# Head of a decoder step: prompt tokens loaded first, their squares on two engines, the new tokens' chain later

## The chip, the cores and the metric

The kernel runs on one core of a Trainium2 chip. The metric is the device time of one execution in microseconds (us); lower is better. A core has a matrix engine (TensorE, here PE, with its weight loads as PEld), a vector engine (VectorE, DVE), an activation engine (ScalarE, ACT), a general engine (GpSimd, POOL) and an engine that mostly issues DMAs (SyncE, SP). Each works through its own queue of instructions in order, and waits at an instruction until the semaphores that this instruction names have come far enough. Matmul results land in PSUM, everything else that the engines read or write lies in SBUF.

## The reference

One layer of a decoder is applied to 512 prompt tokens and to 8 new tokens, 1024 channels each. Only its first lines matter here:

```python
def rms_norm(x, g):
    y = xf * lax.rsqrt(jnp.mean(xf * xf, axis=-1, keepdims=True) + EPS)
    return (y * g.astype(F32)).astype(x.dtype)

def layer_step(r, ...):
    h = rms_norm(r, norm_mix_g)
    z = h @ w_in
    rq, rk, rv, rg, gq, gf, gi, gg, a_ret, a_hg = jnp.split(z, split_at, axis=-1)
    ...
```

Behind this stand a retention branch and an HGRN2 branch, the output projection, an MLP, a gated embedding and a final norm. All of that is the same in both kernels.

## The kernel before

All activations are held transposed, channels on partitions: `xT` (the tokens), and `hH` and `hL`, two parts whose sum is the normalised input h. A float32 matmul is made of three matmuls in a rounded format (fp32r): every operand is cut into a rounded part and a remainder (`hH`, `hL` for activations, `wh`, `wl` for weights), and the product is wh·hH + wh·hL + wl·hH. Eight channel blocks k of 128 and 520 token columns (512 prompt tokens, then the 8 new ones, `T:N`) make up one operand.

The weights come in **units** of 128 output columns: `load()` asks for the next unit's 512 KB (line 237, through SP's queue, into one of three `raw` buffers), and `prep()` cuts it into `wh` and `wl`, in halves or whole, on the engines that its argument names (first the engine of the rounding, then the engine of the subtraction), and asks for a later unit behind that. The program is in the order of the code; no scheduler reorders it.

The change concerns the head, lines 1415 to 1585 or so, up to the third unit:

- **Loads.** SP asks for the identity and ones (`cid`), the new tokens (`xs`, 8 x 1024), a stack of vectors (`rows`, 64 x 128, which holds the gains), and then for the four tiles of 128 prompt tokens (`xn`), with weight units between them.
- **Norm.** `normalized(x, m, c)` squares a tile on ACT and sums each row, forms 1/sqrt by Ln and Exp, and scales the tile on DVE (`xhat`). The new tokens go first, then tiles 0 and 1, later 2 and 3.
- **Transposes.** PE turns the raw tiles (`by_channel`, 4 blocks per PSUM bank; `keep` copies them to `xT` on DVE) and the scaled ones (`hat`, into four banks). `warm` issues transposes of the identity whose result nobody reads. The stack of vectors is turned too and copied to `cv`, whose columns are the gains by channel.
- **Rounding.** `cut(bs, k, half)` makes `hH` for 256 tokens of one block k on ACT, with the gain as scale, and `hL` on DVE.
- **First matmuls.** Units 0 and 1 are done in two halves of tokens (`OFS`: columns 0 to 255, then 256 to 519): `first_z(u, 0, 4)` does the first half of unit u, with the `wl` matmuls four blocks behind the others. Within unit 1's first half PE also turns the scaled tiles 2 and 3, and `cut` follows for the second half. Then both units' second halves run interleaved, with unit 1 two blocks behind.
- From `run_unit` of the third unit on (line 243 in the profile) all 520 columns are done at once.

The PSUM pool `pm` has two buffers of two banks (tiles named `m`). A new tile takes the older buffer, and its first writer waits for the last reader of what was there. Each of units 0 and 1 has one such tile for both its halves (`pp[u]`), so that unit 0 waits for the new tokens' results to be read out of `m0`, and unit 1 for `raws[1]`.

The new tokens' chain is: squares, Ln, Exp, scaling, eight small transposes of `xs` and eight of the scaled tile into `m0`, a copy to `xT`, the gain on DVE (`hd`), and the cut of its columns.

Of the kernel before, what the change touches and what calls it, by code (L numbers as in the profile page):

```python
# [45 lines left out]
def decoder_step_kernel(  # L46
# [1368 lines left out]
    dma(cid, unit_consts)  # L1415
# [4 lines left out]
    xn = []  # L1420
    for c in range(4):
        t = big.tile([128, D], F32, tag=f"S{12 + c}", name=f"xn{c}")
        dma(t, x_prompt[0, c * 128:(c + 1) * 128, :])
        xn.append(t)
        if c > 0:
            load()
# [16 lines left out]
    def normalized(x, m, c):

        r = ss5[0:m, c:c + 1]
        S.activation(junk[0:m], x, AF.Square, accum_out=r)
        S.activation(r, r, AF.Ln, scale=1.0 / D, bias=eps[0:m, 0:1])
        S.activation(r, r, AF.Exp, scale=-0.5)
# [1 line left out]
        V.tensor_scalar(t, x, r, None, op0=ALU.mult)  # L1450
        return t

# [30 lines left out]
    m0 = pm.tile([128, 2, 512], F32, tag="m", name="m")[:, 0]  # L1483
    for k in range(8):
        PE.transpose(m0[:, k * 8:k * 8 + 8], xs[:, k * 128:(k + 1) * 128], ident[0:8, 0:8])
    xh = normalized(xs, 8, 4)
    warm(8, m0[:, 192:320])
    raws = [pm.tile([128, 2, 512], F32, tag="m", name="m")]
# [2 lines left out]
    PE.transpose(m0[:, 128:192], rows, ident[0:64, 0:64])
# [6 lines left out]
    xhat.append(normalized(xn[1], 128, 1))
    keep(0, raws[0][:, 1], 1)
    V.tensor_copy(xT[:, :, T:N], m0[:, 0:64].rearrange("p (k t) -> p k t", k=8))  # L1500
    V.tensor_copy(cv, m0[:, 128:192])
    hd = pair("S1", "hd")[:, 0, 0:64].rearrange("p (k t) -> p k t", k=8)
    V.tensor_tensor(hd, m0[:, 64:128].rearrange("p (k t) -> p k t", k=8),
                    cv[:, V_MIX:V_MIX + 8].unsqueeze(2).to_broadcast([128, 8, 8]), op=ALU.mult)
# [8 lines left out]
    for k in range(8):
        cut(bs, k, 0)
        if k == 3:
            next(p1)
    keep(1, raws[1][:, 0], 0)
    keep(1, raws[1][:, 1], 1)
    xhat.append(normalized(xn[2], 128, 2))
# [148 lines left out]
```

## Time and profile before

| | us |
|---|---|
| median of 3 runs | 1088.36 (1088.34 to 1088.51) |
| the profiled execution | 1088.38 |
| its span, from the first to the last instruction | 1086.6 |
| PE busy in the first 20 us | 16.1 |
| ACT_TABLE_LOAD at the start, on ACT | 1.28 |
| waits of PE that a semaphore ended in the first 40 us, longest | 3.3, for the landing of xs |

The profile names an instruction by the line of the kernel that issued it and by tiles: `hL<-s,cv,hH` writes hL and reads s, cv and hH. A row of the timeline joins equal instructions that follow one another; "x8" is their count, and its time runs from the start of the first to the end of the last. A bracket at its end tells how long the engine had been idle before it and what ended that. PE's matmuls are pipelined, so a matmul's own length is more than the distance to the next one.

### The profile page before, as it was taken

How to read it: one execution, taken by the hardware profiler on the slowest of the kernel's cores; microseconds unless marked ns; L12 is line 12 of the kernel's file. 1: busy time of each engine (PE TensorE's matmuls, PEld its weight loads, DVE VectorE, ACT ScalarE, POOL GpSimd, SP SyncE). 2: the span in 40 equal slices, each digit the busy share in tenths (PEclk: the TensorE clock that was granted, in tenths of full speed). 3: DMA queues.
4: the chain of work that ended last, by engine and by line, in shares of the span. 5: the costliest groups of instructions: out<-in, count | busy, mean ns of one | idle time of the engine just before them, and what ended most of it. 6: DMA issues, size and time to landing. Idle time of an engine off the chain costs nothing.

```text
span 1086.6 us, 23544 instructions
## 1 busy us (share of the span) xinstructions
PE 1075.5 (99%) x10197; PEld 1057.4 (97%) x10197; DVE 685.6 (63%) x1074; ACT 508.4 (47%) x853; POOL 103.3 (10%) x95
## 2 busy tenths in 40 slices
PE   8999999999999999999999999999999999999997
PEld 8999999999999999999999999999999999999997
DVE  6576676858754844775666556855555555554564
ACT  7323534334254333554544345545455445545555
POOL 1000000000011010112222000011121211100001
PEclk9999999999999999999999999999999999999999
DMA  7556253443456355437868533355566665543302
GB/s 224 156 177 176 84 149 91 137 123 87 128 163 176 104 156 166 138 95 177 190 173 196 141 98 83 94 127 145 145 149 154 149 154 143 137 122 113 98 21 79
DMA packets 234952, 147.23 MB, mean 136 GB/s; under 512 B 5320, under 2 KB 229840, under 8 KB 234592
## 3 DMA queue, kind: packets, MB, share of 16 engines
q1 hardware_dynamic: 211600, 125.54, 39.1%
q0 software_dynamic: 23104, 19.93, 10.4%
q8 instruction: 80, 1.31, 0.5%
q10 hardware_dynamic: 144, 0.26, 0.1%
q14 instruction: 24, 0.20, 0.1%
HBM read 131.94 MB, written 13.76 MB: 134 GB/s over the span
## 4 chain that ended last, share of the span: by engine, by line
PE 98%; DVE 1%; ACT 0%; DMA 0%; issue 0%; SPq 0%; DVEq 0%
PE m L243 64%; PE s L881 19%; PE m L1394 2%; PE s L1394 2%; PE s L380 1%; PE s L499 1%; PE s L560 1%; PE s L785 1%; PE s L536 1%; PE s L739 1%; PE s L243 1%; PE s L562 0%; PE s L787 0%; PE s L363 0%; PE s L523 0%; PE s L475 0%
## 5 line engine op out<-in xcount | busy, mean ns | idle before, releaser
L226 DVE TENSOR_TENSOR wl<-raw,wh 128x1024 fp32r<-128x1024 f32 (+1 forms) x125 | 151.8, 1216 | 69.1 <-ACT wh L221 68.3
L243 PE MATMUL m<-hH,wh 128*128 128x260 f32 x864 | 179.1, 289 | 0.0
L243 PE MATMUL m<-hH,wl 128*128 128x260 f32 x864 | 174.4, 283 | 0.0
L243 PE MATMUL m<-hL,wh 128*128 128x260 f32 x864 | 173.7, 283 | 0.0
L221 ACT ACTIVATE wh<-raw 128x1024 fp32r<-128x1024 f32 (+1 forms) x125 | 130.6, 1047 | 78.5 <-PE m L243 61.9
L243 PEld LDWEIGHTS m<-hH,wh 128*128 128x128 f32 x864 | 132.9, 188 | 2.5 <-issue 0.8
L243 PEld LDWEIGHTS m<-hL,wh 128*128 128x128 f32 x864 | 133.1, 188 | 0.0
L243 PEld LDWEIGHTS m<-hH,wl 128*128 128x128 f32 x864 | 133.1, 188 | 0.0
L881 PE MATMUL s<-comb,wh 128*128 128x260 f32 x672 | 122.1, 282 | 0.0
L881 PEld LDWEIGHTS s<-comb,wh 128*128 128x128 f32 x672 | 103.8, 188 | 0.0
L881 PE MATMUL s<-comb,wl 128*128 128x260 f32 x336 | 95.1, 283 | 0.0
L173 ACT ACTIVATE wh<-cst 128x512 fp32r<-128x512 f32 x80 | 50.3, 628 | 52.0 <-DVE cst L179 27.7
L175 DVE TENSOR_TENSOR wl<-cst,wh 128x512 fp32r<-128x512 f32 x80 | 55.2, 690 | 27.4 <-ACT wh L173 26.7
L243 PE MATMUL m<-fa,wh 128*128 128x260 f32 x384 | 66.9, 283 | 0.0
L243 PE MATMUL m<-oga,wh 128*128 128x260 f32 x384 | 64.6, 283 | 0.0
L881 PEld LDWEIGHTS s<-comb,wl 128*128 128x128 f32 x336 | 63.2, 188 | 0.0
L755 POOL TENSOR_TENSOR vbc<-vbc,K 128x1024 f32<-128x1024 f32 x8 | 17.0, 2129 | 409.4 <-DMA vbc<-vdd 409.3
L243 PEld LDWEIGHTS m<-fa,wh 128*128 128x128 f32 x384 | 54.7, 188 | 0.0
L243 PEld LDWEIGHTS m<-oga,wh 128*128 128x128 f32 x384 | 53.7, 188 | 0.8 <-issue 0.8
L1104 DVE TENSOR_TENSOR xT<-xT,m 128x520 f32<-128x520 f32 x32 | 22.3, 696 | 48.4 <-PE m L243 48.4
L243 PE MATMUL m<-fh,wh 128*128 128x260 f32 x256 | 51.5, 282 | 0.0
L243 PE MATMUL m<-fa,wl 128*128 128x260 f32 x256 | 51.5, 283 | 0.0
(396 smaller groups left out, 2439.7 us busy)
## 6 DMA issues: line engine op xcount, KB each, us to landing
raw<-in_w_in_dram SPq DMA_DIRECT2D x56, 512.0 KB, 4.0
...
```

Source lines behind the costliest of these rows:

```text
L173: S.activation(wh[:, 4 * h:4 * h + 4], x, AF.Copy)
L175: V.tensor_sub(wl[:, 4 * h:4 * h + 4], x, wh[:, 4 * h:4 * h + 4])
L221: S.activation(wh[:, k], r[:, k], AF.Copy)
L226: e1.tensor_sub(wl[:, k], r[:, k], wh[:, k])
L243: PE.matmul(ps[z], lhsT=a[:, k, :], rhs=b[:, z * NH:(z + 1) * NH], start=first and i == 0, stop=last and i == 2)
L380: PE.matmul(b[32 * j:32 * j + 32, 32 * hc:32 * hc + 32], lhsT=kx[:, h, o:o + 32], rhs=qx[:, h, o:o + 32], start=True, stop=True)
L499: PE.matmul(b[32 * i:32 * i + 32, :], lhsT=q[g], rhs=Sd[g][:, 4 * z:4 * z + 4, :], start=True, stop=True)
L536: PE.matmul(b[:, c * 128:(c + 1) * 128], lhsT=kn[:, h, c, :], rhs=vn[:, h, c, :], start=True, stop=True)
L755: G.tensor_tensor(t, t, rt["K", P][:, e, T:N].unsqueeze(2).to_broadcast([128, 8, 128]), op=ALU.mult)
L881: PE.matmul(out, lhsT=w[:, 4 * half + k, :], rhs=x, start=start and k == 0 and m == 0, stop=k == 3 and m == 2, skip_group_check=not start)
L1104: V.tensor_tensor(h2(xT[:, j]), h2(xT[:, j]), ps, op=ALU.add)
L1394: PE.matmul(ps, lhsT=w[:, k, :], rhs=x, start=k == 0 and n == 0, stop=k == 7 and n == 2)
```

## The change

The prompt tokens' tiles are asked for first on SP, while ACT's queue asks for `cid`, `rows` and `xs`. The squares of tiles 0 and 1 are split: ACT does channels 0 to 511, DVE the others, and each sums its half; the two sums meet in Ln's scale and bias. The squares of the new tokens are done on DVE. `cv` is filled at the start, behind eight `warm` transposes. The raw tile 1 is turned ahead of the scaled ones, and both raw copies of tile 0 stand ahead of the first `cut`. Both first weight units are cut by POOL alone. The new tokens' scaling stands behind the first `cut` on DVE; their transposes and all that follows (`sample`) stand in unit 1's first half, at k = 2, tile 2's at k = 6, and tile 3's behind it. The two PSUM tiles now each hold one half of the tokens for both units (`pp[z]`), and the new tokens' transposes use free columns of the first (`md`).

```diff
-    dma(cid, unit_consts)
+    S.dma_start(cid, unit_consts)
+    x_load(0)
+    rows = big.tile([64, 128], F32, tag="S10", name="rows")
+    S.dma_start(rows, vecs)
+    x_load(1)
     xs = big.tile([8, D], F32, tag="S11", name="xs")
-    dma(xs, x_sample[:, 0, :])
-    rows = big.tile([64, 128], F32, tag="S10", name="rows")
-    dma(rows, vecs)
...
+    S.dma_start(xs, x_sample[:, 0, :])
+    load()
+    x_load(2)
+    load()
+    x_load(3)
+    load()
     dma(cst, consts)
...
+    def squares_dve(x, m, c0, r):
+        V.scalar_tensor_tensor(junk2[0:m, c0:D], in0=x[:, c0:D], scalar=1.0, in1=x[:, c0:D],
+                               op0=ALU.mult, op1=ALU.mult, accum_out=r)
+
+    def root(r, m, bias):
+        S.activation(r, r, AF.Ln, scale=1.0 / D, bias=bias)
+        S.activation(r, r, AF.Exp, scale=-0.5)
...
+    def root_halves(c):
+        r, b = ss5[:, c:c + 1], ss5[:, 5 + c:6 + c]
+        S.activation(junk[:, 0:512], xn[c][:, 0:512], AF.Square, accum_out=r)
+        squares_dve(xn[c], 128, 512, b)
+        V.tensor_scalar(b, b, 1.0 / D, EPS, op0=ALU.mult, op1=ALU.add)
+        root(r, 128, b)
...
+    m0 = mt()
+    warm(8, m0[:, 1, 0:128])
+    PE.transpose(m0[:, 0, 0:64], rows, ident[0:64, 0:64])
+    V.tensor_copy(cv, m0[:, 0, 0:64])
+    squares_dve(xs, 8, 0, ss5[0:8, 4:5])
+    raws = [mt()]
     for q in range(2):
         by_channel(0, raws[0][:, q], q)
+    root_halves(0)
+    raws.append(mt())
+    for q in range(2):
+        by_channel(1, raws[1][:, q], q)
+    xhat = [normal(xn[0], 128, 0)]
     bs = [bank() for _ in range(4)]
     hat(bs, 0, xhat[0])
+    root_halves(1)
+    xhat.append(normal(xn[1], 128, 1))
+    hat(bs, 1, xhat[1])
+    root(ss5[0:8, 4:5], 8, eps[0:8, 0:1])
+    for q in range(2):
+        keep(0, raws[0][:, q], q)
...
-    p0, p1 = prep([(S, G), (S, G)]), prep([(G, V), (G, V)], apart=True)
+    p0, p1 = prep([(G, G), (G, G)], apart=True), prep([(G, G), (G, G)], apart=True)
     for _ in p0:
         pass
     for k in range(8):
         cut(bs, k, 0)
+    xh = normal(xs, 8, 4)
+    for q in range(2):
+        keep(1, raws[1][:, q], q)
+    for c in (2, 3):
+        r = ss5[:, c:c + 1]
+        S.activation(junk, xn[c], AF.Square, accum_out=r)
+        root(r, 128, eps)
+        xhat.append(normal(xn[c], 128, c))
     for _ in p1:
         pass
...
+    md = pp[0]
+    def sample():
+        for k in range(8):
+            PE.transpose(md[:, 0, 264 + k * 8:272 + k * 8], xs[:, k * 128:(k + 1) * 128], ident[0:8, 0:8])
+        for k in range(8):
+            PE.transpose(md[:, 0, 328 + k * 8:336 + k * 8], xh[:, k * 128:(k + 1) * 128], ident[0:8, 0:8])
+        hd = pair("S1", "hd")[:, 0, 0:64].rearrange("p (k t) -> p k t", k=8)
+        V.tensor_tensor(hd, md[:, 0, 328:392].rearrange("p (k t) -> p k t", k=8),
+                        cv[:, V_MIX:V_MIX + 8].unsqueeze(2).to_broadcast([128, 8, 8]), op=ALU.mult)
+        V.tensor_copy(xT[:, :, T:N], md[:, 0, 264:328].rearrange("p (k t) -> p k t", k=8))
+        S.activation(hH[:, :, T:N], hd, AF.Copy)
+        V.tensor_sub(hL[:, :, T:N], hd, hH[:, :, T:N])
...
-        ps = pp[u][:, z, 0:c1 - c0]
+        ps = pp[z][:, u, 0:c1 - c0]
...
-    first_z(1, 0, 4, {3: 2, 6: 3})
+    first_z(1, 0, 4, {2: sample, 6: lambda: hat(bs, 2, xhat[2])})
+    hat(bs, 3, xhat[3])
```

What this makes of DVE's queue, from the program's start to the first `hL` (its branch and the two instructions behind it left out). Rows give line, instruction, tiles, size and the semaphores waited for. xn_99 and xn_101 are tiles 0 and 1, `ss` the sums. Before:

```order
L1450 TENSOR_SCALAR xhat<-xs,ss_86 8x1024 [waits DMAHW1_49,Activation_49]
L1450 TENSOR_SCALAR xhat<-xn_99,ss_86 128x1024 [waits DMAHW3_49,Activation_49]
L1460 COPY xT<-m 128x4x128 [waits PE_49]
L1450 TENSOR_SCALAR xhat<-xn_101,ss_86 128x1024 [waits DMAHW4_49,Activation_49]
L1460 COPY xT<-m 128x4x128
L1500 COPY xT<-m 128x8x8 [waits PE_49]
L1501 COPY cv<-m 128x64
L1503 TENSOR_TENSOR hd<-m,cv 128x64 [waits DVE_49]
L1480 SCALAR_TENSOR_TENSOR hL<-s,cv,hH 128x256 [waits Activation_49] x8
```

In the changed kernel, where tiles 0 and 1 are xn_95 and xn_99:

```order
L1507 COPY cv<-m 128x64 [waits PE_49]
L1451 SCALAR_TENSOR_TENSOR junk_123,ss_86<-xs 8x1024 [waits DMAHW3_49]
L1451 SCALAR_TENSOR_TENSOR junk_123,ss_86<-xn_95 128x512 [waits DMAHW1_49,DVE_49]
L1468 TENSOR_SCALAR ss_86<-ss_86 128x1 [waits DVE_49]
L1460 TENSOR_SCALAR xhat<-xn_95,ss_86 128x1024 [waits Activation_49]
L1451 SCALAR_TENSOR_TENSOR junk_123,ss_86<-xn_99 128x512 [waits DMAHW4_49]
L1468 TENSOR_SCALAR ss_86<-ss_86 128x1 [waits DVE_49]
L1460 TENSOR_SCALAR xhat<-xn_99,ss_86 128x1024 [waits Activation_49]
L1478 COPY xT<-m 128x4x128 [waits PE_49]
L1478 COPY xT<-m 128x4x128
L1498 SCALAR_TENSOR_TENSOR hL<-s,cv,hH 128x256 [waits Activation_49] x8
```

The copy of cv, which waits for PE, moved from behind both scalings to the head of the queue; three squares and two small scalings are new, and the new tokens' scaling, copy and `hd` are gone from here. Behind this, DVE's queue in the changed kernel goes on from the end of `hL` as follows (xn_105 and xn_109 are tiles 2 and 3):

```order
L1460 TENSOR_SCALAR xhat<-xs,ss_86 8x1024
L1478 COPY xT<-m 128x4x128 x2
L1460 TENSOR_SCALAR xhat<-xn_105,ss_86 128x1024 [waits DMAHW6_49,Activation_49]
L1460 TENSOR_SCALAR xhat<-xn_109,ss_86 128x1024 [waits DMAHW0_49,Activation_49]
L1554 TENSOR_TENSOR hd<-m,cv 128x64 [waits PE_49]
L1556 COPY xT<-m 128x8x8
L1558 TENSOR_TENSOR hL<-hd,hH 128x8x8 [waits Activation_49]
```

There the new tokens' `hd` and the copy out of `md` stand behind the scalings of tiles 2 and 3, where only the last subtraction stood before. On PE, the first half of unit 1 before, from its sixth matmul on:

```order
L1537 MATMUL m<-hL,wh 128x256
L1469 MATMUL s<-cid,xhat 128x128 [waits DVE_49]
L1469 MATMUL s<-cid,xhat 128x128 x7
L1536 MATMUL m<-hH,wh 128x256
L1537 MATMUL m<-hL,wh 128x256
L1536 MATMUL m<-hH,wh 128x256 [waits Pool_49]
```

And the changed kernel's, from unit 1's fourth matmul on:

```order
L1567 MATMUL m<-hL,wh 128x256
L1550 MATMUL m<-cid,xs 128x8 [waits DMAHW3_49]
L1550 MATMUL m<-cid,xs 128x8 x7
L1552 MATMUL m<-cid,xhat 128x8 [waits DVE_49]
L1552 MATMUL m<-cid,xhat 128x8 x7
L1566 MATMUL m<-hH,wh 128x256 [waits DVE_49]
L1567 MATMUL m<-hL,wh 128x256
```

Sixteen small transposes stand there now, and the matmul of line 1566 behind them waits for DVE: for the copy of line 1556, the last of DVE's reads of the PSUM tile into which both the transposes and the matmul write. Before, the matmul at the same place (k = 3, behind tile 2's transposes) waited for nothing.

More of the change, by code (lines that the diff above doesn't have):

```diff
@@ L1412, in run_ple, with x_load @@
         y_last()
-    dma(cid, unit_consts)
-    xs = big.tile([8, D], F32, tag="S11", name="xs")
-    dma(xs, x_sample[:, 0, :])
-    rows = big.tile([64, 128], F32, tag="S10", name="rows")
-    dma(rows, vecs)
[L1420 to L1426, printed above, removed]
+    xn = [None] * 4
+    def x_load(c):
+        xn[c] = big.tile([128, D], F32, tag=f"S{12 + c}", name=f"xn{c}")
+        dma(xn[c], x_prompt[0, c * 128:(c + 1) * 128, :])
+    S.dma_start(cid, unit_consts)
[3 more added lines that the diff above has]
+    x_load(1)
+    xs = big.tile([8, D], F32, tag="S11", name="xs")
+    S.dma_start(xs, x_sample[:, 0, :])
[4 more added lines that the diff above has]
+    load()
     dma(cst, consts)
@@ L1441, in decoder_step_kernel, with normal @@
     junk = big.tile([128, D], F32, tag="S9", name="junk")
[L1443 to L1447, printed above, removed]
+    junk2 = big.tile([128, D], F32, tag="S6", name="junk2")
+    def squares_dve(x, m, c0, r):
[3 more added lines that the diff above has]
+        S.activation(r, r, AF.Ln, scale=1.0 / D, bias=bias)
         S.activation(r, r, AF.Exp, scale=-0.5)
+    def normal(x, m, c):
         t = big.tile([m, D], F32, tag=f"S{3 + c}" if c else "Q", name="xhat")
-        V.tensor_scalar(t, x, r, None, op0=ALU.mult)
+        V.tensor_scalar(t, x, ss5[0:m, c:c + 1], None, op0=ALU.mult)
         return t
+    def root_halves(c):
[4 more added lines that the diff above has]
+        root(r, 128, b)
     def by_channel(c, b, q):
@@ L1481, in cut, with mt @@
                                op0=ALU.mult, op1=ALU.subtract)
[L1483 to L1488, printed above, removed]
+    def mt():
+        return pm.tile([128, 2, 512], F32, tag="m", name="m")
+    m0 = mt()
+    warm(8, m0[:, 1, 0:128])
+    PE.transpose(m0[:, 0, 0:64], rows, ident[0:64, 0:64])
@@ L1496, in decoder_step_kernel @@
+    xhat = [normal(xn[0], 128, 0)]
     bs = [bank() for _ in range(4)]
     hat(bs, 0, xhat[0])
[L1498 to L1504, printed above, removed]
@@ L1511, in decoder_step_kernel @@
-    for q in range(2):
-        by_channel(1, raws[1][:, q], q)
     for k in range(8):
         cut(bs, k, 0)
[L1515 to L1519, printed above, removed]
+    xh = normal(xs, 8, 4)
[6 more added lines that the diff above has]
+        xhat.append(normal(xn[c], 128, c))
@@ L1520, in decoder_step_kernel @@
     for _ in p1:
         pass
-    xhat.append(normalized(xn[3], 128, 3))
-    S.activation(hH[:, :, T:N], hd, AF.Copy)
-    V.tensor_sub(hL[:, :, T:N], hd, hH[:, :, T:N])
     bs = [bank() for _ in range(4)]
-    pp = [pm.tile([128, 2, 512], F32, tag="m", name="m") for _ in range(2)]
+    pp = [mt() for _ in range(2)]
     OFS = ((0, 256), (256, N))
+    md = pp[0]
[10 more added lines that the diff above has]
+        V.tensor_sub(hL[:, :, T:N], hd, hH[:, :, T:N])
@@ L1543, in first_z @@
             if k in mid:
-                hat(bs, mid[k], xhat[mid[k]])
+                mid[k]()
             if k < 8:
```

10 lines of the change are left out of this document (1 added, 9 removed).

## The prediction

> **What bounds the kernel now.** I read the page's shares and its chain of waits first, then the busy time by stretches, then the timeline of the first 27 us.
>
> ```profile
> PE 1075.5 (99%) x10197; PEld 1057.4 (97%) x10197; DVE 685.6 (63%) x1074; ACT 508.4 (47%) x853; POOL 103.3 (10%) x95
> ...
> PE 98%; DVE 1%; ACT 0%; DMA 0%; issue 0%; SPq 0%; DVEq 0%
> ```
>
> TensorE is the chain that ends last. A change that leaves its matmuls alone can only move the moment from which it runs without a break.
>
> ```profile
> 0.00:5.00 5.00, 1.69 (x12) 1.70 (x13) 0.35 (x3) 2.93 (x5) 1.40 (x6) 1.00 0.40 111
> 5.00:10.00 5.00, 4.95 (x31) 3.97 (x29) 2.61 (x4) 3.80 (x10) 0.00 (x0) 1.00 1.06 366
> ...
> 20.00:25.00 5.00, 5.00 (x43) 5.00 (x43) 4.26 (x16) 4.97 (x11) 0.00 (x0) 1.00 0.21 57
> ```
>
> (Columns: stretch, its length, then busy time and count of PE, PEld, DVE, ACT, POOL; granted clock, DMA share, GB/s.) From 20 us PE is full, and no instruction behind the head is changed or moved. So the change is worth what it moves the first matmul of the third unit (line 243). The next rows are of the timeline: start, length, engine, line, work, count.
>
> ```profile
> 0.74 0.39 SPq L1415 DMA_DIRECT2D cid<-in_unit_dram  x1
> ...
> 2.19 1.05 SPq L1423 DMA_DIRECT2D xn<-in_x_prompt_dram  x2
> ...
> 2.86 0.23 DVE L1431 CAST ones_r<-cid 128x128 fp32r<-128x128 f32 x1 [1.99 <-DMA cid<-in_unit_dram]
> ...
> 4.23 1.97 PE L1474 MATMUL m<-cid 128*128 128x128 f32 x8
> ...
> 6.07 1.06 ACT L1446 ACTIVATE junk<-xn 128x1024 f32<-128x1024 f32 x1 [1.17 <-DMA xn<-in_x_prompt_dram]
> ...
> 7.04 0.19 ACT L1446 ACTIVATION_READ_ACCUMULATOR junk<-xn 128x1 f32 x1
> 7.25 0.29 ACT L1447 ACTIVATE ss<-ss,eps 128x1 f32<-128x1 f32 x1
> 7.58 0.20 ACT L1448 ACTIVATE ss<-ss 128x1 f32<-128x1 f32 x1
> ...
> 7.82 0.75 DVE L1450 TENSOR_SCALAR xhat<-xn,ss 128x1024 f32<-128x1024 f32 x1 [2.14 <-ACT ss L1448]
> ...
> 7.99 0.34 PE L1491 MATMUL m<-cid,rows 64*128 64x64 f32 x1
> ...
> 8.48 0.68 DVE L1460 COPY xT<-m 128x512 f32<-128x512 f32 x1
> ...
> 10.23 1.09 PE L1469 MATMUL s<-cid,xhat 128*128 128x128 f32 x8 [0.28 <-DVE xhat L1450]
> ...
> 10.82 0.21 DVE L1501 COPY cv<-m 128x64 f32<-128x64 f32 x1
> ...
> 11.13 3.03 ACT L1479 ACTIVATE hH<-s,cv 128x256 fp32r<-128x256 f32 x8 [0.68 <-PE s L1469]
> ...
> 11.64 3.23 DVE L1480 SCALAR_TENSOR_TENSOR hL<-s,cv,hH 128x256 fp32r<-128x256 f32 x8 [0.35 <-ACT hH L1479]
> ...
> 14.78 1.28 DVE L1460 COPY xT<-m 128x512 f32<-128x512 f32 x2
> ...
> 15.14 0.75 PE L1539 MATMUL m<-hH,wl 128*128 128x256 f32 x5
> ...
> 15.98 0.75 DVE L1450 TENSOR_SCALAR xhat<-xn,ss 128x1024 f32<-128x1024 f32 x1
> ...
> 17.16 0.20 ACT L1448 ACTIVATE ss<-ss 128x1 f32<-128x1 f32 x1
> ...
> 18.81 1.04 PE L1469 MATMUL s<-cid,xhat 128*128 128x128 f32 x8
> ...
> 19.56 3.03 ACT L1479 ACTIVATE hH<-s,cv 128x256 fp32r<-128x256 f32 x8 [2.05 <-PE s L1469]
> ...
> 20.07 3.23 DVE L1480 SCALAR_TENSOR_TENSOR hL<-s,cv,hH 128x256 fp32r<-128x256 f32 x8 [1.34 <-ACT hH L1479]
> ...
> 20.88 0.28 PE L1536 MATMUL m<-hH,wh 128*128 128x264 f32 x1
> ```
>
> ```profile
> 26.74 0.40 PE L243 MATMUL m<-hH,wh 128*128 128x260 f32 x2
> ```
>
> Two points set the head. One is **h**, the start of the first rounding's remainder on DVE (hL): 11.64. The other is what lies from h to the third unit: 26.74 - 11.64 = 15.10. I work out both for the changed order.
>
> **Up to h.** The first tokens are asked for at 0.74 instead of 2.19 and so should land 1.45 earlier than 6.05, at 4.6. But DVE's queue is new ahead of them: it holds the copy of cv, then the squares of the new tokens (8 rows), and only then the tokens' half of the squares. The copy of cv waits for PE's transposition of the vectors, which now stands behind eight warming transposes, and these wait for cid. Before, all that stood beside the tokens' loading, and cv was copied late, at 10.82.
>
> - cid landed at 2.86. The eight warming transposes and the one of the vectors take what eight cold ones and that one took before, from 6.09 (the row of line 1457 is the same form as the 1.97 at 4.23) to 7.99 + 0.34, so 2.24. With 0.10 of semaphores and 0.21 for the copy, DVE is free at **S** = 5.41.
> - cid now comes by ACT's queue beside the tokens' 512 KB. Bounds: nothing, and the whole tile first (512 KB at 366 GB/s, 1.4). I take 0.3, nearly the 0.36 of its own 128 KB at that rate, as both flow together: S = 5.7. rows and xs, behind it on ACT, were asked for at 0.4 us steps and are covered by the warming; ACT's table load too, since ACT first works at 4.6.
> - No squares on DVE are in the trace. The nearest:
>
> ```profile
> L756 DVE SCALAR_TENSOR_TENSOR rSd<-rSd,vbc x8: 1218/1220/2920, 321.8 to 448.8; 128x1024 f32<-128x1024 f32 x8
> L226 DVE TENSOR_TENSOR wl<-raw,wh x125: 692/1225/1228, 16.6 to 1032.8; 128x1024 fp32r<-128x1024 f32 x123, 128x512 fp32r<-128x512 f32 x2
> 25.08 0.16 DVE L1568 TENSOR_SCALAR lbv<-lbv 128x8 f32<-128x8 f32 x1
> ```
>
>   So 1.22 for 1024 elements and 0.70 for 512. Reading the sum cost ACT 0.18; on DVE it may cost nothing to 0.18; I take 0.18.
> - From S: squares of xs 1.40, gap 0.03, half squares 0.88, the small scaling 0.03 + 0.16, Ln 0.05 + 0.29, Exp 0.04 + 0.20, 0.04: the first scaling of tokens starts at S + 3.12. It gives way to the next instruction after 0.66 (7.82 to 8.48). The second tile repeats 0.88 + 0.19 + 0.34 + 0.24 + 0.04: its scaling starts at S + 5.47 and ends 0.75 later. Then 0.06 to its transposes, 0.75 from there to hH (18.81 to 19.56), 0.51 to hL: h = S + 7.54. The two copies of xT, now ahead of hL, need 0.66 + 1.20 and are ready a little sooner. ACT's half squares lie beside DVE's.
> - So h = 5.7 + 7.5 = 13.25 without a collision.
>
> **POOL's port.** Both first weight units are now rounded by POOL alone: four casts and four subtractions, from the landing of the first weights (about 8.2: third on SP, after two tiles), against two and two before:
>
> ```profile
> 10.01 2.53 POOL L226 TENSOR_TENSOR wl<-raw,wh 128x512 fp32r<-128x512 f32 x2 [8.08 <-ACT wh L221]
> ...
> 12.49 1.16 POOL L223 CAST wh<-raw 128x512 fp32r<-128x512 f32 x2
> ...
> 405.13 1.23 DVE L226 TENSOR_TENSOR wl<-raw,wh 128x1024 fp32r<-128x1024 f32 x1 [0.25 <-ACT wh L221]
> 405.88 2.23 POOL L755 TENSOR_TENSOR vbc<-vbc,K 128x1024 f32<-128x1024 f32 x1 [0.63 <-DMA vbc<-vdd]
> 406.27 2.92 DVE L756 SCALAR_TENSOR_TENSOR rSd<-rSd,vbc 128x1024 f32<-128x1024 f32 x1
> ```
>
> A unit costs POOL 2.53 + 1.16 = 3.7, so both end at 15.6 or a little later; PE needs the last piece after that, hence POOL is not the bound by itself. But the last row is the long one among eight (1.22 usual): an operation with two SBUF inputs on DVE waited 1.70 for POOL's subtraction to end. The second half square, at S + 3.78 = 9.5, falls into POOL's first subtraction (8.8 to 10.1): **0.6**. Bounds: 0 if they miss each other, 2.3 if the two scalings are held as well (1.27 for a subtraction, 0.58 for a cast, and part of another). I take 0.6, since only operations with two inputs are seen to wait. h = 13.85, 2.2 later than before.
>
> [...]
>
> **From h to the third unit.** The eight transposes of xs and the eight of its scaled copy stand in the middle of unit 1's first half, and the next matmul waits for DVE's copy out of that tile (a wait for the tile's reader, although it goes to another bank). On DVE that copy stands behind the hL chain, the scaling of xs, two copies of xT and the scalings of token tiles 2 and 3.
>
> - DVE from h: 3.14 (11.64 to 14.78), 0.66, 1.20 (14.78 to 15.98), 0.66 = 5.66. The scaling of tile 3 needs ACT's Exp, at 17.36 - 11.64 = 5.72 from hL as before, so 5.76; then 0.66, 0.13, 0.21 and 0.15 to PE: PE goes on at h + 6.9.
> - PE was done with unit 0 at 15.14 + 0.75 = h + 4.2; four matmuls and 16 small transposes (1.2) bring it to h + 5.8. So it stands for 1.1 us.
> - Then 20 matmuls of 0.118 (2.4), and the transposes of tiles 2 and 3, 0.8 each. Tile 3's stand last: they start at h + 10.05. From them to hH 0.75, to hL 0.51, to the matmul 0.45: before, eleven matmuls lay over this. The second half's 48 matmuls take 5.86 (20.88 to 26.74) from hH's 11.3, and 0.45 for the first hL: h + 17.6, against 15.1. **+2.5**.
>
> What PE no longer does ahead of unit 0 (four warming transposes, the second tile's eight) gains nothing: its unit 0 ends 0.9 after the last hL (14.87) in both. Loads of later weights are asked for earlier and nobody waits for them.
>
> **Sum.** 2.2 + 2.5 = 4.7 on the profiled run's 1088.38 (span 1086.6 and 1.8 around it; the median is 1088.36): **1093.1 us**.
>
> **Rivals.**
>
> - *Not slower: the tokens' landing is the bound, as the edit's order supposes.* If cv and the squares of xs are done by 4.6, h is 4.6 + 7.54 - 1.43 = 10.7, 0.9 earlier; with +2.5 that gives 1.6, 1090.0, within 0.2% (2.2 us, about what a measurement of this kernel tells from no change). It decides at a cv copied by 3.2, so a cid at 0.7; shorter squares could do part of it. Against it: cid at 2.86 and 1.97 for eight transposes. Chance 0.09. To be faster by 2.2, h would have to be 6.9, only 2.3 behind the tokens' landing, with two scalings in it; 0.03 for what I haven't seen.
> - *The port holds scalings too:* 2.3 instead of 0.6, 1094.8. Chance 0.28.
> - *No collision, no cost for the sum's reading* (h 0.6 and 0.5 earlier): 1092.0. Chance 0.2.
> - *PE goes slow again.* At 4.23 eight transposes took 1.97, at 10.23 1.09. In the new order PE has only 16 transposes between about 8.5 and 13.5. Matmuls at twice 0.118 would take 24 x 0.12 = 2.9 more, of which the 1.1 us stand hides a part: 1094.9. For it speaks that PE became fast only after some 5 us of work (3.3 to 8.9 in the trace); against it, that no gap of the new order is longer than the 3 us that I find between the two tiles' transposes. Chance 0.1.
>
> The forecast itself has 0.3. Range: cid at its upper bound (+1.1) with the port's upper bound (+1.7) gives 1095.9; below, no collision and no reading gives 1092.0, and 1.0 less for squares that I priced too high, 1091.0. Faster 0.03, same 0.09, slower 0.88.
>
> **What would show it.** In the changed trace: DVE's first half square starts behind the squares of xs, at about 7, not at the landing; hL starts at 13 to 15; a gap on PE before the third pair of unit 1, ended by DVE's copy of xT; a second gap after tile 3's transposes, ended by hH; POOL's subtractions and DVE's second half square not side by side. Wrong if hL starts before 11.3, or if the 15.10 does not grow by over 2.

## The result, and the profile after

| | before | changed |
|---|---|---|
| median of the runs on one chip, us | 1088.53 (1088.34 to 1089.68, 6 runs) | 1096.9 (1095.86 to 1097.48, 6 runs) |
| ratio to before | 1 | 1.0073 [1.006, 1.0086] |
| profiled execution, its span | 1088.38, 1086.6 | 1097.45, 1095.7 |
| start of the third unit on PE (line 243) | 26.74 | 36.02 |

The change made the kernel slower, by 8.4 us in the medians and 9.1 between the profiled executions, where 4.7 was predicted. The sign was right; the time lies 1.0 above the range. On every chip the kernel before has single runs near 1088.3 and near 1089.6, with a few above, so a difference of 1 us between its medians means nothing. The page of the changed kernel has the same outline as before: PE is the chain that ends last.

```profile
PE 1079.1 (98%) x10193; PEld 1059.8 (97%) x10193; DVE 690.2 (63%) x1080; ACT 505.4 (46%) x849; POOL 107.8 (10%) x99
...
PE 98%; DVE 1%; DMA 0%; ACT 0%; issue 0%; DVEq 0%; ACTq 0%
```

So the loss is again to be looked for ahead of the third unit, and there it is, whole: its start moved by 9.28. The busy time by stretches (columns as in the prediction; the granted clock is the third number from the right) tells where PE stood and where it was slow; the row by itself is the kernel before's.

```profile
0.00:5.00 5.00, 0.00 (x0) 0.00 (x0) 0.06 (x1) 1.28 (x1) 1.40 (x6) 1.00 0.59 170
5.00:10.00 5.00, 4.41 (x20) 3.97 (x21) 2.31 (x5) 0.72 (x2) 0.73 (x2) 1.00 1.10 334
10.00:15.00 5.00, 2.74 (x16) 2.15 (x15) 3.61 (x9) 1.99 (x8) 4.92 (x4) 0.96 1.16 351
15.00:20.00 5.00, 5.00 (x22) 4.44 (x22) 4.27 (x11) 3.88 (x10) 3.27 (x4) 0.50 0.82 273
```

```profile
15.00:20.00 5.00, 4.68 (x41) 4.51 (x40) 3.73 (x7) 2.82 (x11) 0.00 (x0) 1.00 1.03 344
```

PE does nothing at all in the first 5 us (12 matmuls before), it stands for nearly half of the stretch from 10 to 15, and from 15 to 20 it is "busy" throughout with 22 matmuls where the kernel before did 41: its clock was granted at 0.50. (The clock's column alone does not tell how fast PE is: it reads 1.00 from 5 to 10 too, where eight transposes took 1.97. The rows' own lengths must be read beside it.) The timeline of the changed kernel gives the steps (start, length, engine, line, work; the bracket is the idle time before and what ended it).

```profile
5.36 0.63 ACT L1466 ACTIVATE junk<-xn 128x512 f32<-128x512 f32 x1 [1.59 <-DMA xn<-in_x_prompt_dram]
...
5.57 0.23 DVE L1437 CAST ones_r<-cid 128x128 fp32r<-128x128 f32 x1 [4.70 <-DMA cid<-in_unit_dram]
5.59 1.97 PE L1492 MATMUL m<-cid 128*128 128x128 f32 x8 [5.59 <-DMA cid<-in_unit_dram]
...
7.89 0.23 DVE L1507 COPY cv<-m 128x64 f32<-128x64 f32 x1 [2.10 <-PE m L1506]
8.03 1.20 DVE L1451 SCALAR_TENSOR_TENSOR junk<-xs 8x1024 f32<-8x1024 f32 x1
...
9.28 1.07 DVE L1451 SCALAR_TENSOR_TENSOR junk<-xn 128x512 f32<-128x512 f32 x1
...
11.20 0.82 DVE L1460 TENSOR_SCALAR xhat<-xn,ss 128x1024 f32<-128x1024 f32 x1 [0.66 <-ACT ss L1456]
...
11.94 1.09 DVE L1451 SCALAR_TENSOR_TENSOR junk<-xn 128x512 f32<-128x512 f32 x1
...
13.88 0.82 DVE L1460 TENSOR_SCALAR xhat<-xn,ss 128x1024 f32<-128x1024 f32 x1 [0.66 <-ACT ss L1456]
...
14.76 1.97 PE L1487 MATMUL s<-cid,xhat 128*128 128x128 f32 x8 [1.59 <-DVE xhat L1460]
...
16.63 3.23 DVE L1498 SCALAR_TENSOR_TENSOR hL<-s,cv,hH 128x256 fp32r<-128x256 f32 x8 [0.73 <-ACT hH L1497]
...
23.66 0.23 DVE L1554 TENSOR_TENSOR hd<-m,cv 128x64 f32<-128x64 f32 x1 [0.52 <-PE m L1552]
...
24.07 0.39 PE L1566 MATMUL m<-hH,wh 128*128 128x256 f32 x1 [0.45 <-DVE xT L1556]
...
27.43 1.04 PE L1487 MATMUL s<-cid,xhat 128*128 128x128 f32 x8
...
28.17 3.03 ACT L1497 ACTIVATE hH<-s,cv 128x256 fp32r<-128x256 f32 x8 [3.99 <-PE s L1487]
28.68 3.23 DVE L1498 SCALAR_TENSOR_TENSOR hL<-s,cv,hH 128x256 fp32r<-128x256 f32 x8 [4.24 <-ACT hH L1497]
28.70 0.39 PE L1566 MATMUL m<-hH,wh 128*128 128x264 f32 x1 [0.24 <-ACT hH L1497]
```

```profile
36.02 0.51 PE L243 MATMUL m<-hH,wh 128*128 128x260 f32 x2 [0.75 <-ACT f L1614]
```

Three things are to be seen. The identity (`cid`) lands at 5.5, 2.7 later than before, with the first tile of tokens at its side, so all that hangs on it is late: PE's transposition of the vectors, the copy of cv, the squares. Tile 1's eight transposes take 1.97 at 14.76, twice the 1.04 of the eight at 27.43. And the third unit's first matmul waits 0.75 for ACT's activations `f`, a wait that the kernel before doesn't have.

Against the prediction's steps the 9.28 divide so: S (DVE free after the copy of cv) at 8.03 instead of 5.7, **+2.33**; from S to h 8.60 instead of 8.15, **+0.45**; from h to the second halves' first hL 12.05 instead of 11.3 (10.05, 0.75 and 0.51; the prediction calls this point hH's, but its terms lead to hL), **+0.74**; from there to the third unit 7.34 instead of 6.31 (5.86 and 0.45), **+1.03**.

### The profile page after: what moved, and what is told of

Same layout as the page of the kernel before. It is cut to its first block, busy times and chain, and to the rows that moved or that the text cites. A ratio compares the mean times of both kernels' runs of the same rounds, so it can differ in the third digit from the quotient of the medians.

```text
span 1095.7 us, 23537 instructions
## 1 busy us (share of the span) xinstructions
PE 1079.1 (98%) x10193; PEld 1059.8 (97%) x10193; DVE 690.2 (63%) x1080; ACT 505.4 (46%) x849; POOL 107.8 (10%) x99
## 4 chain that ended last, share of the span: by engine, by line
PE 98%; DVE 1%; DMA 0%; ACT 0%; issue 0%; DVEq 0%; ACTq 0%
PE m L243 63%; PE s L881 18%; PE m L1394 2%; PE s L1394 2%; PE s L380 1%; PE s L499 1%; PE s L536 1%; PE s L560 1%; PE s L785 1%; PE s L739 1%; PE s L243 1%; PE s L562 0%; PE s L787 0%; PE m L1567 0%; PE m L1566 0%; DMA cid<-in_unit_dram 0%
## 5 line engine op out<-in xcount | busy, mean ns | idle before, releaser
L226 DVE TENSOR_TENSOR wl<-raw,wh 128x1024 fp32r<-128x1024 f32 x123 | 152.6, 1241 | 68.8 <-ACT wh L221 68.1
L221 ACT ACTIVATE wh<-raw 128x1024 fp32r<-128x1024 f32 x123 | 129.5, 1053 | 79.1 <-PE m L243 62.1
L243 PE MATMUL m<-fl,wh 128*128 128x260 f32 x256 | 51.4, 282 | 0.0
```

The source lines that it names most:

```text
L221: S.activation(wh[:, k], r[:, k], AF.Copy)
L226: e1.tensor_sub(wl[:, k], r[:, k], wh[:, k])
L243: PE.matmul(ps[z], lhsT=a[:, k, :], rhs=b[:, z * NH:(z + 1) * NH], start=first and i == 0, stop=last and i == 2)
```

## The experiments

In twelve kernels single parts of the change were undone or done alone. The table has the medians, and from each trace the start of the first hL, the stand of PE ahead of the matmul behind the new tokens' transposes, and the start of the third unit. Rows in bold letters carry the argument; the kernel before had medians of 1089.55 (e1 to e4), 1088.48 (e5, e7, e9, b1) and 1089.47 (the others) on the same chips.

| kernel | median us | first hL | PE's stand | third unit |
|---|---|---|---|---|
| before | 1088.5 | 11.64 | none | 26.74 |
| **the changed one** | 1096.9 | 16.63 | 0.45 | 36.02 |
| e1 small loads first on SP | 1095.55 | 13.15 | 1.89 | 34.41 |
| **e2 cid alone on ACT** (one run) | 1095.46 | 12.98 | 1.86 | 34.21 |
| e3 f in the tiles' order | 1095.57 | 16.37 | 0.45 | 34.39 |
| e4 PE kept busy | 1097.27 | 15.87 | 1.02 | 36.26 |
| **e5** e2, reads first | 1092.51 | 12.97 | 0.54 | 31.24 |
| e7 e2, squares later (one run) | 1094.38 | 13.62 | 0.45 | 33.15 |
| e9 before, new loads (one run) | 1094.06 | 17.76 | none | 32.84 |
| **e10** e5, f in order | 1091.50 | 13.16 | 0.54 | 30.49 |
| **e11** e10, tile 3 earlier | 1090.71 | 13.09 | 0.54 | 29.64 |
| **e12** e11, unit 0 by ACT | 1089.96 | 12.65 | 0.45 | 29.07 |
| b1 before, split squares | 1089.70 | 12.26 | none | 27.36 |
| b3 b1 mended | 1089.51 | 12.69 | none | 28.34 |

### The loads: e2, e1, e9

The theory is that cid was late because it shared the DMA engines with two tiles; its rival, that ACT's queue itself is slow.

```diff
 e2
     S.dma_start(cid, unit_consts)
...
+    dma(rows, vecs)
...
+    dma(xs, x_sample[:, 0, :])
     x_load(0)
...
-    S.dma_start(rows, vecs)
     x_load(1)
...
-    S.dma_start(xs, x_sample[:, 0, :])
 e1: as e2, and
-    S.dma_start(cid, unit_consts)
+    dma(cid, unit_consts)
```

> The changed kernel with cid still asked for by ACT, but rows and xs by SP ahead of the tiles, so that the first tile is asked for at about 1.6 and cid has the engines to itself for almost a microsecond. Theory A (sharing): cid lands at 2.9 to 3.2. Rival C (a load on ACT's queue takes some 4.8 us whatever else runs): cid lands at about 5.5 again.

> The changed kernel with cid, rows and xs asked for by SP ahead of the first token tile, as before, and nothing else. Theory A (the small loads, on ACT's queue, share the DMA engines with the tiles that SP asks for at the same moment, so cid lands at 5.5 and rows at 7.2 instead of 2.9 and 3.6, and DVE's queue stands behind them): cid lands at 2.9, cv is copied at about 5.3 instead of 7.9, hL starts 2 to 2.6 us earlier (14.0 to 14.6), the time falls by 2 to 2.6 us to about 1094.5. Rival B (h is set by the token tiles' landing or by POOL's port): the tiles land 1.4 us later, hL starts no earlier, the time stays within 0.8 us of the changed kernel's.

The timeline of e2:

```profile
2.90 0.23 DVE L1437 CAST ones_r<-cid 128x128 fp32r<-128x128 f32 x1 [2.03 <-DMA cid<-in_unit_dram]
...
5.57 0.63 ACT L1466 ACTIVATE junk<-xn 128x512 f32<-128x512 f32 x1 [3.14 <-DMA xn<-in_x_prompt_dram]
...
12.98 3.23 DVE L1498 SCALAR_TENSOR_TENSOR hL<-s,cv,hH 128x256 fp32r<-128x256 f32 x8 [0.18 <-ACT hH L1497]
...
16.12 1.70 DVE L1460 TENSOR_SCALAR xhat<-xs,ss 8x1024 f32<-8x1024 f32 x1
...
20.66 0.39 PE L1566 MATMUL m<-hH,wh 128*128 128x256 f32 x1 [1.86 <-DVE xT L1556]
...
22.11 1.91 PE L1487 MATMUL s<-cid,xhat 128*128 128x128 f32 x8
```

On the same queue, with only small loads beside it, cid lands at 2.9 instead of 5.5, and the tile of tokens still lands at 5.6, no more than 0.2 later than when it was asked for first. So ACT's queue is not slow, and asking for the tiles ahead bought 0.2 in the changed kernel (0.7 to 0.9 in e3 and e4 below, where the tile landed at 4.70 and 4.84), which DVE could not use. The views of DMA issues say the same of the vectors (KB, us from issue to landing), in the changed kernel and then in e2:

```profile
rows<-in_vecs_dram ACTq DMA_DIRECT2D x1, 32.0 KB, 6.0
```

```profile
rows<-in_vecs_dram SPq DMA_DIRECT2D x1, 32.0 KB, 2.3
```

A second queue gave the 32 KB no way past the tiles: 6.0 from issue to landing on ACT beside them, against 2.3 on SP ahead of them. In what turns the two queues were served is not shown: cid, with 128 KB, landed 0.2 behind the whole first tile (in e3 and e4 too).

But of the 3.65 that h gained in e2, only 1.8 reached the third unit: PE now stands 1.86 for DVE's copy, and slow matmuls follow it. e1 is the same with cid on SP (cid at 2.7, hL at 13.15), and for the same reason it gained 1.35 instead of the 2 to 2.6 expected. e9 puts the new loads alone into the kernel before.

```diff
 e9: the kernel before, with the changed kernel's loads
-    dma(cid, unit_consts)
+    S.dma_start(cid, unit_consts)
+    x_load(0)
...
```

> The kernel before with nothing but the changed kernel's order and queues of the loads. Theory A (the small loads on ACT's queue beside the tiles land at 5 and 7 to 8 us): cid at about 5, xs at about 7.8, and as ACT squares xs first there, hL starts at 14.5 to 15 instead of 11.64 and the time grows by 2.5 to 3.5 us. Rival K (the earlier tokens make up for it): hL at 11.6 or before, time within 0.5 us.

```profile
5.02 0.23 DVE L1437 CAST ones_r<-cid 128x128 fp32r<-128x128 f32 x1 [4.16 <-DMA cid<-in_unit_dram]
...
8.29 1.06 ACT L1452 ACTIVATE junk<-xs 8x1024 f32<-8x1024 f32 x1 [4.50 <-DMA xs<-in_x_sample_dram]
...
17.76 3.23 DVE L1486 SCALAR_TENSOR_TENSOR hL<-s,cv,hH 128x256 fp32r<-128x256 f32 x8 [2.25 <-ACT hH L1485]
```

The loads alone cost the kernel before 5.6 us in its one run, about twice what was expected. The old order begins with `xs`, which here landed 6.5 us after it was asked for (at 1.76), while the new one begins with cid. That explains a part only: hL is some 3 us later than the expectation had it with xs at 7.8, and PE's transposes are slow behind xs (sixteen of the scaled tiles span 3.67 from 14.18).

### The wait for f: e3

Each PSUM tile holds one half of the tokens for both units now, but ACT still reads unit by unit: first half and second half of unit 0, then unit 1. So the last read of the first halves' tile, which the third unit takes over, stands behind a read of the second halves.

```diff
-    for u in range(2):
-        for z, (c0, c1) in enumerate(OFS):
...
+    for z, (c0, c1) in enumerate(OFS):
+        for u in range(2):
             S.activation(st["f", 0][:, u, c0:c1], pp[z][:, u, 0:c1 - c0], AF.Tanh, scale=0.5)
...
```

> The changed kernel with the four activations of f in the order of the PSUM tiles: both units' first halves, then both second halves. Theory D (the third unit's first matmul waits 0.75 us because its PSUM buffer, the first halves' tile, is read out third, behind an activation that waits for the end of both second halves): the first matmul of line 243 follows the last of line 1569 within 0.15 us, and the time falls by 0.7 to 0.9 us. Rival E (the wait is hidden by, or moves to, the weights or another buffer of that unit): it starts no earlier than now, time within 0.3 us.

```profile
34.39 0.40 PE L243 MATMUL m<-hH,wh 128*128 128x260 f32 x2
```

The wait is gone and the median 1.3 lower than the changed kernel's. Not all of that is the 0.75: in this execution the second halves' hL starts 0.7 earlier too, at 27.96. e10 below measures the edit by itself.

### PE's slow stretch: e4

Twenty warming transposes fill PE's gaps ahead of and behind tile 0's scaled transposes.

```diff
+    warm(6, bs[3][:, 128:256])
     hat(bs, 0, xhat[0])
+    warm(14, bs[3][:, 128:256])
     root_halves(1)
```

> The changed kernel with 20 more transposes of the identity that nobody reads, 6 ahead of the first tile's scaled transposes and 14 behind them, in PE's idle time. Theory F (PE's clock falls to half between 14.8 and 21.9 because PE idles at 11.4 and 13.2 us; the trace shows 0.50 granted): PE stays fast, the second tile's transposes take 1.1 instead of 1.97, hL starts 0.6 to 0.9 earlier, unit 0's matmuls follow at 0.12, the time falls by 0.9 to 1.6 us. Rival G (the slow stretch is hidden behind DVE's queue, which releases the matmul behind the new tokens' transposes): hL a little earlier, time within 0.5 us.

```profile
14.56 1.09 PE L1487 MATMUL s<-cid,xhat 128*128 128x128 f32 x8
...
22.70 0.39 PE L1568 MATMUL m<-hH,wh 128*128 128x256 f32 x1 [1.02 <-DVE xT L1558]
...
24.12 1.91 PE L1487 MATMUL s<-cid,xhat 128*128 128x128 f32 x8
```

Tile 1's transposes are fast and hL starts 0.76 earlier, 0.2 of it ahead of tile 1's scaling, since the loads landed earlier in this execution (cid at 5.01). But the time is as before the edit: the rival came. PE reaches the new tokens' transposes sooner, stands there 1.02 for DVE, and the slow stretch comes behind that stand. Filling the first gap only moved the cost to the next: DVE's queue sets the pace, and the clock follows (granted 0.88 from 20 to 25 and 0.78 from 25 to 30).

### DVE's queue in unit 1: e5 and e7

If the stand is due to `hd` and the copy of xT lying behind two scalings that nobody waits for yet, then moving the reads ahead takes it away. e5 does so, on top of e2. e7, also on e2, leaves that order and puts the new tokens' squares behind tile 1's scaling.

```diff
 e5
-        xhat.append(normal(xn[c], 128, c))
...
         V.tensor_copy(xT[:, :, T:N], md[:, 0, 264:328].rearrange("p (k t) -> p k t", k=8))
+        xhat.append(normal(xn[2], 128, 2))
         S.activation(hH[:, :, T:N], hd, AF.Copy)
         V.tensor_sub(hL[:, :, T:N], hd, hH[:, :, T:N])
+        xhat.append(normal(xn[3], 128, 3))
 e7
-    squares_dve(xs, 8, 0, ss5[0:8, 4:5])
...
     hat(bs, 1, xhat[1])
+    squares_dve(xs, 8, 0, ss5[0:8, 4:5])
```

> As e2 (cid on ACT, rows and xs on SP ahead of the tiles), and the two reads of md by DVE stand ahead of the scalings of token tiles 2 and 3, not behind them. In e2 PE stands 1.86 us at the matmul behind the new tokens' transposes and then runs 2.1 to 2.9 us at half speed. Theory H (the stand is set by the two scalings in DVE's queue, and the slow stretch follows from the stand): PE goes on at about 19.4 instead of 20.66, no slow stretch or a shorter one, the third unit starts 1.2 to 2.3 us earlier than in e2 (34.21). Rival I (the next wait, for ACT's sums of tiles 2 and 3 at the transposes of tile 2, takes its place): under 0.5.

> As e2, and the squares of the new tokens stand behind the scaling of tile 1 on DVE, not ahead of tile 0's. Theory J (DVE's queue ahead of the tiles is on the path to hL): the first scaling starts at about 7.0 instead of 8.16 and the second at 9.1 to 9.6 instead of 10.78; of this hL keeps 0.3 to 0.8 (12.2 to 12.7 instead of 12.98), because the squares now stand ahead of the copies of xT. Rival B (POOL's port or the landing sets it): the second scaling starts within 0.4 of 10.78.

The timeline of e5, and its stretch from 20 to 25 us:

```profile
19.33 0.39 PE L1567 MATMUL m<-hH,wh 128*128 128x256 f32 x1 [0.54 <-DVE xT L1555]
...
23.94 3.23 DVE L1498 SCALAR_TENSOR_TENSOR hL<-s,cv,hH 128x256 fp32r<-128x256 f32 x8 [3.21 <-ACT hH L1497]
```

```profile
20.00:25.00 5.00, 4.63 (x38) 4.19 (x37) 1.79 (x5) 1.56 (x5) 0.00 (x0) 1.00 0.12 31
```

With the first hL at the same 12.97, the second halves' hL starts at 23.94 instead of 26.86, and the third unit 2.97 earlier, more than the 1.2 to 2.3 expected: 1.3 less stand, and the rest goes with the slow stretch that no longer follows it (clock 1.00 here, 0.67 in e2). This is the largest single step of the mending, though e2, from which it is counted, has one run. In e7 both scalings start as early as expected (7.32 and 9.52), and the timeline shows why its first hL is later all the same:

```profile
10.19 2.29 DVE L1451 SCALAR_TENSOR_TENSOR junk<-xs 8x1024 f32<-8x1024 f32 x1
...
12.53 0.29 ACT L1455 ACTIVATE ss<-ss,eps 8x1 f32<-8x1 f32 x1 [3.03 <-DVE junk L1451]
...
13.62 3.20 DVE L1498 SCALAR_TENSOR_TENSOR hL<-s,cv,hH 128x256 fp32r<-128x256 f32 x8
```

The squares fall beside POOL's subtraction and cast (9.60 to 12.96), take 2.29 instead of 1.20, and ACT's queue holds hH back behind the Ln that waits for them. The gain of 1.1 against e2 is no proof of the move: the stand of 1.86 shrank to 0.45 because the later start left PE late as well.

### The sum: e10, e11, e12

e10 is e5 with e3's edit. e11 adds tile 3's transposes at a place with matmuls behind them. e12 adds the rounding of unit 0's weights by ACT, as in the kernel before.

```diff
 e11
-    first_z(1, 0, 4, {2: sample, 6: lambda: hat(bs, 2, xhat[2])})
-    hat(bs, 3, xhat[3])
+    first_z(1, 0, 4, {2: sample, 5: lambda: hat(bs, 2, xhat[2]), 7: lambda: hat(bs, 3, xhat[3])})
 e12
-    p0, p1 = prep([(G, G), (G, G)], apart=True), prep([(G, G), (G, G)], apart=True)
+    p0, p1 = prep([(S, G), (S, G)]), prep([(G, G), (G, G)], apart=True)
```

> The changed kernel with four small loads in the order of e5 (cid by ACT alone, rows and xs ahead of the tiles), DVE's reads of the new tokens' PSUM tile ahead of the scalings of tiles 2 and 3, and the activations f taken tile by tile as in e3. Theory: PE's 0.76 us stand ahead of line 243 adds to the rest, since PE is full behind it: 0.7 to 0.8 under e5's 1092.5, so 1091.8, and line 243 starts at 30.5 without a wait. Rival: the wait only goes over to another reader or to the end of the second halves, 1092.5 again.

> As e10, and tile 2's transposes at k = 5 and tile 3's at k = 7 of unit 1's first half instead of k = 6 and behind everything, as in the kernel before where matmuls stand behind tile 3's transposes. Theory: tile 3 standing last costs PE the time from its transposes to the first hL (in e5 0.24, 0.33 and the 0.75 between), about 1.0 to 1.2: 1090.7, and no wait for hH before the first matmul of the second halves. Rival: PE then waits for the scaling of tile 3 on DVE (ready at about 20.8 in e5) instead, and only 0.3 or less is gained: 1091.5 or more.

> As e11, but unit 0's weights are rounded by ACT and subtracted by POOL, as in the kernel before; unit 1 stays with POOL. Theory of the shared port: with no cast on POOL beside it DVE's second half square goes back from 1.1 to 0.7 and hL starts about 0.35 earlier, 12.6 instead of 13.0; ACT has 1.1 free for the rounding: 1090.3 against 1090.7 of e11. Rival: the square's length is not POOL's doing, it stays at 1.1, and the time is e11's or up to 0.5 later because ACT's rounding stands ahead of hH.

e10 came out 0.3 under its theory's 1091.8, and its third unit starts 0.75 earlier than e5's without a wait, though the second halves' hL is 0.18 later (24.12); e5 waited 0.76 there. e11 hit its 1090.7, by luck: it gained 0.8 on e10, where 1.0 to 1.2 were expected, from a start 0.3 lower. The third unit moved by 0.85, so tile 3 standing last did cost, a little less than was thought. What the prediction calls POOL's port shows on tile 1's scaling, first in e11 (DVE, then POOL beside it), then in e12 (DVE, then POOL):

```profile
10.21 1.51 DVE L1460 TENSOR_SCALAR xhat<-xn,ss 128x1024 f32<-128x1024 f32 x1 [0.66 <-ACT ss L1456]
```

```profile
9.91 1.26 POOL L226 TENSOR_TENSOR wl<-raw,wh 128x512 fp32r<-128x512 f32 x1
11.12 1.07 POOL L223 CAST wh<-raw 128x512 fp32r<-128x512 f32 x1
```

```profile
10.38 0.75 DVE L1460 TENSOR_SCALAR xhat<-xn,ss 128x1024 f32<-128x1024 f32 x1 [0.66 <-ACT ss L1456]
```

```profile
11.37 2.51 POOL L226 TENSOR_TENSOR wl<-raw,wh 128x512 fp32r<-128x512 f32 x2 [9.44 <-ACT wh L221]
```

In e11 POOL's subtraction is under way when DVE issues the scaling, and the scaling ends 0.5 after it, at 11.7. In e12 POOL starts only at 11.37, and the same scaling takes 0.75. The expectation had named the wrong instruction: the second half square was at 0.69 in e11 already, because it started ahead of POOL's work (8.67 against 8.74). But that an instruction of DVE lasts longer beside POOL's subtraction is shown, 1.51 against 0.75, and e12 gains 0.75 in the median, more than the 0.4 it was given; the third unit moved by 0.57.

e12 at 1089.96 is the best of the changed order, 1.0009 [1.0, 1.0018] of the kernel before: no measurable difference, or a small loss, but no gain.

### The parts that might have helped: b1, b3

b1 takes into the kernel before what the new order promised, without its costs: small loads ahead of the tiles with cid on ACT, tile 0's squares on both engines, an early cv. b3 splits tile 1's squares as well and puts warming ahead of the new tokens' transposes.

```diff
 b1
-    dma(cid, unit_consts)
+    S.dma_start(cid, unit_consts)
...
-    xhat = [normalized(xn[0], 128, 0)]
+    xhat = [normalized_split(xn[0], 0)]
 b3: as b1, and
+    raws = [pm.tile([128, 2, 512], F32, tag="m", name="m")]
+    warm(4, raws[0][:, 0, 0:128])
...
-    xhat.append(normalized(xn[1], 128, 1))
+    xhat.append(normalized_split(xn[1], 1))
```

> A version of the kernel before, made from what the runs show: cid on ACT's queue with only rows and xs beside it, the first tile asked for at 1.6; tile 0's squares split over ACT and DVE, tile 1's on ACT alone (so that they run beside DVE's scaling of tile 0); cv copied at the start; all else as before (new tokens' chain in the loading time, POOL's share of the weights as before). By the rows: tile 0 lands at 5.6 instead of 6.07, its scaling starts at 7.1 instead of 7.82, tile 1's at 8.7 instead of 9.42, hL at 10.8 instead of 11.64, the 15.10 behind it unchanged: 0.8 us faster than the kernel before, 0.07%. If PE's clock sets in later than in the kernel before, nothing is gained.

> The kernel before with cid by ACT, rows and xs on SP, the squares of tiles 0 and 1 split over ACT and DVE, cv filled early, and four warming transposes ahead of the new tokens', four behind, in the raw tile's PSUM buffer so that they do not wait for DVE's copy of cv. Theory: b1 gained nothing although tile 0 landed earlier because PE was still slow at 7.4 to 9.3 (its eight transposes took 1.91) and its warming waited for the copy of cv; with both mended hL starts at 11.0 to 11.3 instead of 12.26 in b1 and 11.64 before: 1087.5 to 1088.1. Rival: the second tile's chain on ACT or the copies out of PSUM on DVE bind, hL at 11.6 to 12.2: 1088.4 to 1089.0.

Neither is faster: ratios of 1.0003 [0.9994, 1.0012] and 1.0009 [1.0, 1.0018]. The timeline of b3 and its stretch from 10 to 15 us:

```profile
5.51 0.63 ACT L1456 ACTIVATE junk<-xn 128x512 f32<-128x512 f32 x1 [0.20 <-DMA xn<-in_x_prompt_dram]
...
10.34 0.75 DVE L1464 TENSOR_SCALAR xhat<-xn,ss 128x1024 f32<-128x1024 f32 x1 [0.66 <-ACT ss L1462]
...
11.14 1.64 PE L1483 MATMUL s<-cid,xhat 128*128 128x128 f32 x8 [1.53 <-DVE xhat L1464]
...
12.69 3.23 DVE L1494 SCALAR_TENSOR_TENSOR hL<-s,cv,hH 128x256 fp32r<-128x256 f32 x8 [0.73 <-ACT hH L1493]
```

```profile
10.00:15.00 5.00, 3.86 (x21) 3.86 (x21) 3.93 (x10) 4.13 (x12) 3.66 (x4) 0.66 1.14 351
```

Tile 0 lands 0.5 earlier than before and is worked on at once, yet tile 1's scaling starts at 10.34 where the chain on ACT alone had it at 9.42. Its split squares stand on DVE behind the copy of xT, at 8.80. Then PE has stood for 1.53 and is slow again. The rival, that tile 1's chain binds, is what came in kind; hL at 12.69 is later than the 12.2 it allowed. Why the split does not pay for tile 0 follows from the rows: from the start of ACT's square to the scaling it takes 2.02 in b3 (5.51 to 7.53) and 2.18 in b1 (5.64 to 7.82), the undivided chain 1.75 (6.07 to 7.82). ACT saves 0.4 (1.06 to 0.63) and DVE pays 0.67, a reading of 0.07, a scaling of 0.15 and a hand-over to ACT of 0.10.

## Why the prediction was right in sign and short in size

**Right:** the bound (everything ahead of the third unit), the sign, and the reason for it, that DVE's queue starts with a copy that hangs on cid through PE, not with the tokens. The tokens landed at 5.3 instead of 6.05, though not at the 4.6 taken; ACT squared its half at once, and DVE came to its own at 9.28. The rival on the other side needed cv to be copied by 3.2; it was copied at 7.9. Of the signs named, both gaps on PE are there (0.45 at 24.07, ended by the copy of xT; 0.24 at 28.70, ended by hH). The first half square starts at 9.28 instead of about 7, and hL at 16.63 instead of 13 to 15: both carry the same 2.3, hL 0.45 more. The last sign came in part: DVE's second half square (11.94 to 13.03) starts behind one of POOL's subtractions, but the next lies beside it from 12.56.

**Wrong, cid's delay** (the step "cid now comes by ACT's queue beside the tokens' 512 KB"): 0.3 taken, 1.4 as the upper bound, 2.7 measured. The 0.3 let both flow together, and the bound let cid wait for one tile. But SP had asked for two of them by 1.6 us; 1 MB at the prediction's own 366 GB/s takes 2.9, and that bound would have held. It is no rule that the runs show: SP had asked for a weight unit and a third tile too (1.66 and 2.12) before cid landed, and with the same loads cid landed at 4.9 to 5.0 in e3, e4 and e9, 2.0 to 2.2 late. There xs, on the same queue, came late as well: in e3 and e4 DVE waited for it and began its squares at 7.85 and 7.89. S = 5.41 + 2.7 is 8.1, against 8.03 measured. This is the largest miss, +2.33, and e2, in which cid lands at 2.9 and S is at 5.36, shows it to be the loads and nothing else. That h came back by 3.65 in e2, more than 2.33, has two other parts: tile 1's transposes were fast there (1.10 against 1.97), and POOL's rounding fell on other instructions (the first half square took 0.69 against 1.07).

**Nearly right, DVE from S to h.** From S to the first scaling 3.17, predicted 3.12 plus the collision; the reading of a sum on DVE cost 0.07 to 0.11 rather than 0.18, the squares of xs 1.20. The collision came on both half squares (1.07 and 1.09, 0.69 when POOL is idle, as in e2 at 6.61) and little on the scalings (0.82). The chain without PE's part is 0.16 shorter than predicted. The rival that the port holds scalings came in e11 (1.51, against 0.75 in e12). Its 2.3 was an estimate from the lengths of POOL's rows, and no run shows it: in the changed kernel both scalings began only 0.27 before the end of a subtraction, ended 0.55 behind it, as e11's did, and took 0.82. In e1 and e2 the scaling of xs took 1.7.

The delay goes in both directions: scalings of 1.51 (e11) and 1.70 (e2) on DVE, against 0.75 (e12) and 0.73 (xs in the changed kernel), and on POOL the first two rows of the changed kernel below, beside DVE's half squares and scalings, against the last two, beside DVE's hL (which reads PSUM and one tile in SBUF). By what the two engines hold each other up no run shows; the port is the prediction's name for it.

```profile
9.88 1.59 POOL L226 TENSOR_TENSOR wl<-raw,wh 128x512 fp32r<-128x512 f32 x1
...
11.41 1.07 POOL L223 CAST wh<-raw 128x512 fp32r<-128x512 f32 x1
...
16.46 0.61 POOL L223 CAST wh<-raw 128x512 fp32r<-128x512 f32 x1
...
17.15 1.28 POOL L226 TENSOR_TENSOR wl<-raw,wh 128x512 fp32r<-128x512 f32 x1
```

**Wrong, PE's clock** (the rival with 0.1). It was argued away by the length of the gaps: none over 3 us. That such gaps leave the clock alone was my estimate, and no run shows it: the clock fell after gaps of 0.67 and 1.59. Its share on the path is 0.61 at tile 1's transposes (from their start to hH 1.36, 14.76 to 16.12, predicted 0.75; 0.81 in e4, where they are fast); behind that unit 0's matmuls ran at 0.21 instead of 0.12 until about 21.9, most of it under DVE's queue, of which 0.52 came through (`hd` waited that long for PE). It should have been a term beside the others, not a rival to them; the range's upper end, added up from cid and the port, had left its 1.8 out.

**Right in kind, the stand for DVE's copy.** Predicted 1.1, measured 0.45, because PE itself was late; in e1 and e2, where PE is on time, 1.9. Its true price is with its consequence: e5 gains 3.0 by removing it, the slow stretch included. The term was sized without the clock.

**Wrong by omission, the third unit's own start** (the step "The second half's 48 matmuls take 5.86 (20.88 to 26.74)"). Of the 1.03 there, 0.75 is the wait for f: the exchange of `pp[u]` for `pp[z]` was described as a change of layout, and I didn't ask which read of the first tile is the last. The remaining 0.3 is the pace of the matmuls behind hL. Of the 0.74 ahead of it, 0.52 is the clock's share named above and 0.2 the matmuls and transposes from 24.07 to 27.43.

With S, the clock and the wait put right (2.33, 1.1 and 0.75) the sum of 4.7 becomes 8.9, of 9.28. With all of this mended the changed order (e12) still reaches the third unit 2.3 later than the kernel before. 1.0 of it is h. For the rest, 1.3, the timeline of e12 gives an account that no run tests by itself: the new tokens' sixteen transposes and the stand behind them hold PE for 1.6 within unit 1 (17.32 to 18.92), work that the kernel before does while it waits for tokens, and against that unit 1 starts 4.1 behind hL instead of 4.6. What is not settled is what lies behind the third unit: it took 1059.2 in e12's profiled execution and 1059.9 in that of the kernel before, so that the spans differ by 1.7 only.
